# Hybrid decoder layer on one core: all projections first, then attention and output projection of the next 512 tokens emitted between the feed-forward of the current 512

## The chip, the cores and the metric

The kernel runs on one core of one Trainium2 chip. The metric is device time in microseconds (us), the median of several runs. Engines are called as the profile calls them: PE is TensorE, PEld its weight loads, DVE is VectorE, ACT is ScalarE, POOL is GpSimd, SP is SyncE, which here issues all DMAs.

## The reference

One layer over 2048 tokens of width 1024, in float32:

```python
h = rmsnorm(x, norm_mix);  proj = h @ w_in                  # 1024 x 2048
a_u, a_v, b_in, c_q, c_k, c_v, d_q, d_k, d_v = split(proj)
y_a = chunked_sgu(a_u, a_v)              # gating inside 128-token chunks
y_b = multiscale_pool(b_in)              # trailing means of 2, 4, 8, 16 tokens
y_c = sliding_window_attention(c_q, c_k, c_v)      # window 128, sinks, bias
y_d = stick_breaking_attention(d_q, d_k, d_v)      # causal, over all 2048 keys, 4 heads of 64
x = x + rmsnorm_per_mixer(concat(y_a, y_b, y_c, y_d)) @ w_out     # 1024 x 1024
h = rmsnorm(x, norm_ffn);  gate, up = split(h @ w_gate_up)         # 1024 x 5632
x = x + (silu(gate) * up) @ w_down                                 # 2816 x 1024
return rmsnorm(x, norm_final)
```

Stick-breaking weights are `sigmoid(z_ts)` times the product of `1 - sigmoid(z_tj)` over the keys between s and t: a running product along the keys, from the newest to the oldest.

## The kernel before, in words

Every product of two matrices is made of three matmuls: each operand is split into a high part and a low remainder (hi and lo), and hi*hi, hi*lo and lo*hi are summed in one PSUM bank. The split of a tile is a copy on ACT and a subtraction on POOL or DVE.

**Mixers (first 1070 us of the trace).** Three streams are written as Python generators, and `merge` (L687) emits pieces of a second stream between pieces of the first by a table of ratios (L863). The main stream is `stick` (L288): stick-breaking attention for one chunk of 512 queries and one pair of heads, eight calls. `weights` makes one block of 128 queries against 512 keys: two matmuls into a bank `z` (L300, L301), two sigmoids on ACT into `tfix` and `s` (L304, L307), a scan on DVE (L313) into `pr`, and a product `s` (L318). `turn` transposes one block of 128 keys of four such blocks (L328) into a bank `tr`, and splits it (ACT L330, DVE L331). `values` multiplies it with the values (L339, L340) into `acc`. Six `s` buffers, and two banks each for `z` and `tr`. The stream in between is `feed` (L732): projections of keys and queries of two heads, values, pooling, then the second pair of heads, spatial gating, and the third mixer's projections. Keys (`kstack`) and values (`vstack`) stay in SBUF for all 2048 tokens. After the eight calls, sliding-window attention `swa` (L419) and `out_proj` (L636) are emitted together; `out_proj` reads each 128-token tile of the mixers' results back from DRAM (`y<-yd`), norms, transposes (`ytr`) and multiplies it with the output weights, which `load_wo` (L607) splits once.

**Feed-forward (from 1070 us on).** Two blocks of 1024 tokens (L938). For each of 22 slices `f` of 128 hidden channels: `fsplit` (L904) loads and splits three weight tiles of 512 KB (`fraw`, two buffers, then `fw` in a ring of eight), 96 matmuls make gate and up (`gu`, L950), ACT and DVE form the activation (L970 to L974), and after every second slice 96 matmuls multiply with w_down (`dn`, L985) and DVE adds them to the residual `xa` (L986). `hT`, the normed tokens transposed and split, is kept for 1024 tokens.

The order on each engine is fixed when the program is built: a scheduler (`schedule_with_timeline_sim=True`) takes the emitted instructions and may take a later one first when an earlier one waits. On the chip each engine runs its list in that order.

The lines that decide where things lie:

```python
w = sb.tile([P, CH], F32, name="s", tag="dq" if spare_q else "s", bufs=4 if spare_q else 6)      # L306
ratios = (38 / 10.8, 38 / 21.6, 38 / 32.4, 52 / 43.2, 4.00, 1.20, 1.00, 1.50)                    # L863
merge(stick(c, pair, q[n]), upto(n + 2 if n < 6 else 99), ratios[n])                             # L871
ring = top.enter_context(tc.tile_pool(name="ring", bufs=8, side="left", reuse_waits="tile"))     # L874
raw = ring.tile([P, D], F32, name="fraw", tag="raw", bufs=2)                                     # L905
for blk in range(T // TB):                                                                       # L938
```

Of the kernel before, what the change touches and what calls it, by code (L numbers as in the profile page):

```python
# [15 lines left out]
P = 128  # L16
# [16 lines left out]
# column ranges of w_in  # L33
# [35 lines left out]
def _layout(inputs):  # L69
    """The arrays as the kernel reads them: slices, transposes and tiles of the inputs."""  # L70
# [33 lines left out]
TB = 1024  # L104
NT = TB // P
KS = NCH + 1
ON_G = [(7, 3)]
# [7 lines left out]
def _build(nc, tc, A, top):  # L115
    V, S, G = nc.vector, nc.scalar, nc.gpsimd
# [5 lines left out]
    dram = top.enter_context(tc.tile_pool(name="dram", bufs=1, space=bass.MemoryType.DRAM))  # L122
    yd = [dram.tile([SUB, D], F32, name=f"yd{s}") for s in range(NS)]
    vd = [dram.tile([CH, 256], F32, name=f"vd{c}") for c in range(NCH)]
    x2d = [dram.tile([CH, D], F32, name=f"x2d{c}") for c in range(NCH)]
    hn = [dram.tile([P, D], F32, name=f"hn{i}") for i in range(NT)]
    biasd = dram.tile([4, P, 384], F32, name="biasd")
    cd = [dram.tile([3, P, SUB], F32, name=f"cd{s}") for s in range(NS)]
    rbcd = [dram.tile([P, SUB], F32, name=f"rbcd{s}") for s in range(NS)]

# [5 lines left out]
    ones = const.tile([P, P], F32, name="ones")  # L136
# [8 lines left out]
    def normed(pool, x, g, out):  # L145
        """out = x * rstd(x) * g; out is scratch until then."""
        ss = pool.tile([P, 1], F32, name="fss", tag="fss", bufs=2)
        S.activation(out, x, AF.Square, accum_out=ss)
        r = pool.tile([P, 1], F32, name="fr", tag="fr", bufs=2)
        rstd(r, ss, D, pool)  # L150
        V.scalar_tensor_tensor(out, x, r, g, op0=ALU.mult, op1=ALU.mult)

    psum = top.enter_context(tc.tile_pool(name="psum", bufs=2, space=PSUM))
    rx = const.tile([P, NB], F32, name="rx")

    with ExitStack() as ph1:
        c1 = ph1.enter_context(tc.tile_pool(name="c1", bufs=1, side="left"))
        sb = ph1.enter_context(tc.tile_pool(name="sb", bufs=2, side="left"))

        stack = c1.tile([P, HD], F32, name="stack")  # L160
        tfix = [c1.tile([P, CH + 1], F32, name=f"tfix{i}") for i in range(2)]
        for t in tfix:
            G.memset(t[:, CH:CH + 1], 1.0)
        tcount = [0]
        kstack = [c1.tile([P, KS, CH], F32R, name=f"kstack{h}") for h in range(2)]
        vstack = c1.tile([P, NB, 2, P], F32R, name="vstack")

# [1 line left out]
        spare = []  # L169

        def raw_tile(shape, name):
            if spare and name == "wraw":
                tag, n = spare.pop(0)
                return sb.tile(shape, F32, name=name, tag=tag, bufs=n)
            return pp.tile(shape, F32, name=name, tag="raw", bufs=3)

        def stats(s):
            """rstd of the 256 tokens of sub-chunk s: a column of rx a block, and a row on all partitions."""
            ss = pp.tile([P, 2], F32, name="ss")
            for i in range(2):  # L180
                b = 2 * s + i
                xt = raw_tile([P, D], "xt")
                load(xt, A["x"][b * P:(b + 1) * P, :])
                S.activation(xt, xt, AF.Square, accum_out=ss[:, i:i + 1])
            r = rx[:, 2 * s:2 * s + 2]
            rstd(r, ss, D, pp)
            bc = psum.tile([P, CH], F32, name="bc", tag="ms", bufs=1)
            for i in range(2):
                dg = pp.tile([P, P], F32, name="dg", tag="k1")
                V.tensor_scalar(dg, ident, rx[:, 2 * s + i:2 * s + i + 1], None, op0=ALU.mult)  # L190
                nc.tensor.matmul(bc[:, i * P:(i + 1) * P], ones, dg, start=True, stop=True)
            rbc = pp.tile([P, SUB], F32, name="rbc", tag="rbc", bufs=2)
            S.copy(rbc, bc[:, :SUB])
            load(rbcd[s], rbc)
            return rbc

        def stored_stats(s):
            rbc = pp.tile([P, SUB], F32, name="rbc", tag="rbc", bufs=2)
            load(rbc, rbcd[s])
            return rbc  # L200

        def make_h(s, on_v=()):
            """The 256 tokens of sub-chunk s: two tiles of four channel blocks, hi and lo."""
            tok = slice(s * SUB, (s + 1) * SUB)
            out = []
            for q in range(2):
                xr = raw_tile([P, 4, SUB], "xr")
                load(xr, A["xT"][q * CH:(q + 1) * CH, tok].rearrange("(k p) t -> p k t", p=P))
                h = pp.tile([P, 4, 2, SUB], F32R, name="h", tag="h", bufs=4)
                S.copy(h[:, :, 0], xr)  # L210
                (V if q in on_v else G).tensor_tensor(h[:, :, 1], xr, h[:, :, 0].bitcast(F32), op=ALU.subtract)  # L211
                out.append(h)
            return out

# [1 line left out]
        def split_w(src, name, tag="w", bufs=4, eng=G, k0=0, step=KT):  # L216
            """src: channel blocks k0 on of [P, k, n] in DRAM; returns the hi and lo tile [P, 2, k, n]."""
            _, kt, n = src.shape
            w = (fa if tag == "wv" else pp).tile([P, 2, kt, n], F32R, name=name, tag=tag, bufs=bufs)
            per = min(kt, D // n, step)  # L220
            for k in range(0, kt, per):
                raw = raw_tile([P, per, n], "wraw")
                load(raw, src[:, k:k + per])
                g = gmix[:, k0 + k:k0 + k + per].rearrange("p (k o) -> p k o", o=1).broadcast_to([P, per, n])
                V.tensor_tensor(raw, raw, g, op=ALU.mult)
                S.copy(w[:, 0, k:k + per], raw)
                eng.tensor_tensor(w[:, 1, k:k + per], raw, w[:, 0, k:k + per].bitcast(F32), op=ALU.subtract)
            return w

        banks = ["mm", "mm", "z", "z", "tr", "tr"]  # L230

        def bank_of():
            return psum.tile([P, CH], F32, name="ps", tag=banks.pop(0) if banks else "mm")

        def proj_cm(h, w):
            ps = bank_of()
            o = ps[:, :SUB]
            for k in range(KT):
                hk = h[k // 4][:, k % 4]
                nc.tensor.matmul(o, w[:, 0, k], hk[:, 0], start=k == 0, stop=False)  # L240
                nc.tensor.matmul(o, w[:, 0, k], hk[:, 1], start=False, stop=False)  # L241
                nc.tensor.matmul(o, w[:, 1, k], hk[:, 0], start=False, stop=k == KT - 1)  # L242
            return o

        def proj_tm(h, w, n, i):
            """w(k, u): the hi (u = 0) or lo columns of channel block k."""
            ps = bank_of()
            o = ps[:, :n]
            t = slice(i * P, (i + 1) * P)
            for k in range(KT):  # L250
                hk = h[k // 4][:, k % 4, :, t]
                nc.tensor.matmul(o, hk[:, 0], w(k, 0), start=k == 0, stop=False)  # L252
                nc.tensor.matmul(o, hk[:, 0], w(k, 1), start=False, stop=False)  # L253
                nc.tensor.matmul(o, hk[:, 1], w(k, 0), start=False, stop=k == KT - 1)
            return o

# [1 line left out]
        def scaled(ps, rbc):  # L258
            t = pp.tile([P, SUB], F32, name="sc", tag="k1")
            V.tensor_tensor(t, ps, rbc, op=ALU.mult)  # L260
            return t

        def dup_q(t, outs, cols):
            """[hi; hi] and [lo; lo] of both heads in a channel-major pair."""
            for h in range(2):
                q = outs[h]
                r = slice(h * HD, h * HD + HD)
                o = slice((1 - h) * HD, (1 - h) * HD + HD)
# [19 lines left out]
        def stick(c, pair, q):  # L288
# [45 lines left out]
            def values(h, j, kb, r, wt):  # L334
# [6 lines left out]
                if j == 0 and kb == 3:  # L341
                    finish(h)
# [669 lines left out]
```

## Time and profile before

| what | value |
|---|---|
| device time, median of 3 runs | 2550.84 us (2548.78 to 2551.43) |
| profiled execution, span from first to last instruction | 2542.3 us |
| what lies around the span (median less span) | 8.5 us |
| PE busy | 2381.7 us (94%), 11836 matmuls |
| DVE, ACT, POOL busy | 1313.0 us (52%), 827.2 us (33%), 670.3 us (26%) |
| chain that ended last: PE, DVE, DMA, issue, ACT | 70%, 15%, 5%, 4%, 3% |
| mean granted TensorE clock | 0.971 |
| HBM read, written | 162.31 MB, 36.44 MB |

The profiled execution's own device time is not listed beside its span; the 8.5 us are taken from the median of the runs. A "busy" PE is one whose matmuls' modelled spans cover the time: matmuls overlap, so the distance from one start to the next says what a matmul costs, not its duration.

### The profile page before, as it was taken

To read this page: it belongs to the slowest core of one execution; us is meant where nothing else is said; L and a number is where in the kernel's file an instruction comes from. 1 tells how busy PE (TensorE), PEld (TensorE's weight loads), DVE (VectorE), ACT (ScalarE), POOL (GpSimd) and SP (SyncE) were. 2 spreads that over 40 slices of the span, in tenths; PEclk is the share of its full clock that TensorE was granted. 3 is DMA by queue.
4 is the path that set the end of the run, shared out by engine and by line. 5 is a ranking of instruction groups with operands and counts; after the bars stand their busy time and mean duration, and the time that the engine had idled before them with its cause. 6 is when DMAs were issued, how large, how long until landed. Compare 5 with 4: busy or idle time off the path is not lost.

```text
span 2542.3 us, 30367 instructions
## 1 busy us (share of the span) xinstructions
PE 2381.7 (94%) x11836; PEld 2003.2 (79%) x11836; DVE 1313.0 (52%) x2010; ACT 827.2 (33%) x1708; POOL 670.3 (26%) x504
## 2 busy tenths in 40 slices
PE   6989798887986889999999999999999999999998
PEld 6978677776865777888888888888788888888886
DVE  6788999898874554233333333333533333333335
ACT  5465566664653443222221111112411111111112
POOL 4232444553421211132222122222211222222210
PEclk9989999998996999999999999999999999999999
DMA  6241311222214333342221111111611111111101
GB/s 209 65 132 64 101 44 32 62 73 92 92 41 156 107 110 130 137 177 84 83 88 45 50 50 50 50 50 47 219 35 49 50 50 50 50 50 43 49 25 67
DMA packets 100480, 200.72 MB, mean 79 GB/s; under 512 B 8656, under 2 KB 64368, under 8 KB 100336
## 3 DMA queue, kind: packets, MB, share of 16 engines
q1 hardware_dynamic: 100336, 198.78, 23.7%
q8 instruction: 93, 1.52, 0.2%
q14 instruction: 51, 0.42, 0.1%
HBM read 162.31 MB, written 36.44 MB: 78 GB/s over the span
## 4 chain that ended last, share of the span: by engine, by line
PE 70%; DVE 15%; DMA 5%; issue 4%; ACT 3%; POOL 2%; SPq 0%; POOLq 0%; DVEq 0%; ACTq 0%
PE gu L950 38%; PE dn L985 19%; DVE pr L313 4%; DVE s L318 2%; PE ops L676 2%; PE ops L677 2%; PE ops L678 2%; DVE wt L331 1%; PE ps L240 1%; PE ytr L628 1%; PE ps L242 1%; PE ps L241 1%; PE ps L252 1%; PE ps L253 1%; ACT block L465 1%
## 5 line engine op out<-in xcount | busy, mean ns | idle before, releaser
L950 PE MATMUL gu<-hT,fw 128*128 128x512 f32 x4224 | 992.6, 390 | 0.0
L950 PEld LDWEIGHTS gu<-hT,fw 128*128 128x128 f32 x4224 | 792.5, 188 | 166.7
L909 POOL TENSOR_TENSOR fw<-fraw,fw 128x1024 fp32r<-128x1024 f32 x132 | 315.6, 2397 | 1033.0 <-ACT fw L908 1033.0
L985 PE MATMUL dn<-fw,act 128*128 128x512 f32 x2112 | 525.8, 395 | 1.4 <-DVE xa L986 0.8
L986 DVE TENSOR_TENSOR xa<-dn,xa 128x512 f32<-128x512 f32 x352 | 240.6, 689 | 551.4 <-PE dn L985 550.9
L985 PEld LDWEIGHTS dn<-fw,act 128*128 128x128 f32 x2112 | 394.8, 188 | 97.8 <-DVE xa L986 2.3
L908 ACT CAST fw<-fraw 128x1024 fp32r<-128x1024 f32 x132 | 138.6, 1053 | 562.3 <-issue 342.1
L970 ACT ACTIVATE sg<-gu 128x512 f32<-128x512 f32 x88 | 48.0, 595 | 549.4 <-PE gu L950 549.4
L972 DVE TENSOR_TENSOR sg<-gu,sg 128x512 f32<-128x512 f32 x88 | 56.7, 683 | 222.3 <-PE gu L950 222.3
L211 POOL TENSOR_TENSOR h<-xr,h 128x1024 fp32r<-128x1024 f32 x47 | 122.3, 2611 | 110.8 <-ACT h L210 108.4
L974 DVE TENSOR_TENSOR act<-sg,act 128x512 fp32r<-128x512 f32 x88 | 129.9, 1514 | 23.8 <-ACT act L973 23.6
L313 DVE TENSOR_TENSOR_SCAN pr<-tfix,cr 128x513 f32<-128x513 f32 x96 | 134.3, 1406 | 11.2 <-ACT tfix L304 11.0
L971 DVE TENSOR_TENSOR sg<-gu,sg 128x512 f32<-128x512 f32 x88 | 56.9, 686 | 121.7 <-ACT sg L970 121.6
L318 DVE TENSOR_TENSOR s<-s,pr 128x512 f32<-128x512 f32 (+3 forms) x152 | 117.1, 780 | 5.1 <-ACT s L307 1.2
L328 PE MATMUL tr<-ident,s 128*128 128x128 f32 x544 | 95.2, 279 | 12.8 <-DVE wt L331 7.1
L676 PE MATMUL ops<-wo,yT 128*128 128x512 f32 x256 | 102.1, 400 | 2.0 <-ACT yT L630 1.8
L677 PE MATMUL ops<-wo,yT 128*128 128x512 f32 x256 | 101.2, 395 | 0.0
L304 ACT ACTIVATE tfix<-z 128x512 f32<-128x512 f32 (+3 forms) x160 | 86.0, 538 | 45.0 <-PE z L301 31.9
L678 PE MATMUL ops<-wo,yT 128*128 128x512 f32 x256 | 100.4, 396 | 0.0
L330 ACT CAST wt<-tr 128x512 fp32r<-128x512 f32 (+3 forms) x160 | 81.8, 530 | 56.4 <-PE tr L328 53.2
L331 DVE TENSOR_TENSOR wt<-tr,wt 128x512 fp32r<-128x512 f32 (+3 forms) x160 | 93.3, 597 | 9.5 <-ACT wt L330 9.0
L328 PEld LDWEIGHTS tr<-ident,s 128*128 128x128 f32 x544 | 68.8, 143 | 25.5 <-issue 9.0
(194 smaller groups left out, 3523.2 us busy)
## 6 DMA issues: line engine op xcount, KB each, us to landing
fraw<-in_w_gu SPq DMA_DIRECT2D x88, 512.0 KB
xr<-in_xT SPq DMA_DIRECT2D x48, 512.0 KB
fraw<-in_w_down SPq DMA_DIRECT2D x44, 512.0 KB
xt<-in_x SPq DMA_DIRECT2D x16, 512.0 KB
xres<-in_x SPq DMA_DIRECT2D x16, 512.0 KB
y<-yd SPq DMA_DIRECT2D x16, 512.0 KB
x2d<-xres SPq DMA_DIRECT2D x16, 512.0 KB
xa<-x2d SPq DMA_DIRECT2D x16, 512.0 KB
```

The costliest lines, as they stand in the source:

```text
L313: V.tensor_tensor_scan(pr[:, c0:][:, ::-1], t[:, c0:][:, ::-1], t[:, c0:][:, ::-1], carry[h][i], op0=ALU.mult, op1=ALU.bypass)
L318: (G if (4 * pair + c, i) in ON_G else V).tensor_tensor(w[:, c0:], w[:, c0:], pr[:, c0 + 1:], op=ALU.mult)
L328: nc.tensor.transpose(tr[:, i * P:(i + 1) * P], wq[i][:, col:col + P], ident)
L676: nc.tensor.matmul(ps, yk[:, 0, :], wo[k][:, 0, cs], start=k == 0, stop=False)
L677: nc.tensor.matmul(ps, yk[:, 0, :], wo[k][:, 1, cs], start=False, stop=False)
L678: nc.tensor.matmul(ps, yk[:, 1, :], wo[k][:, 0, cs], start=False, stop=k == KT - 1)
L908: S.copy(w[:, 0], raw)
L909: G.tensor_tensor(w[:, 1], raw, w[:, 0].bitcast(F32), op=ALU.subtract)
L950: nc.tensor.matmul(pss[u][n], ws[u][:, wi, sl], hT[:, k, hi, n * CH:(n + 1) * CH], start=k == 0 and wi == 0 and hi == 0, stop=k == KT - 1 ...
L974: V.tensor_tensor(a[n][:, 1], sg, a[n][:, 0].bitcast(F32), op=ALU.subtract)
L985: nc.tensor.matmul(ps, l, r, start=j == 0, stop=j == len(m) - 1)
L986: V.tensor_tensor(xa[i][:, cs], ps, xa[i][:, cs], op=ALU.add)
```

## The change

- Keys, queries and values of all four heads of stick-breaking attention are projected in one first pass over the tokens, with pooling, and go to DRAM (`kd`, `qd`, `vv`). A second pass projects the sliding-window operands and makes spatial gating. Nothing of the attention is emitted in the first pass; attention of the first 512 tokens is merged into the second pass.
- `attention(c)` is sliding-window attention (`swa`) and both pairs of `stick` for 512 tokens; it fetches keys, queries and values from DRAM (`kst`, `dq`, `vst`, two buffers each).
- `out_proj(c)` takes 512 tokens at a time and loads and splits the output weights again for each chunk, from the feed-forward's ring.
- The feed-forward runs over four chunks of 512 tokens in place of two blocks of 1024, so its weights are loaded and split four times. Between its pieces `merge` emits `attention(c + 1)` and `out_proj(c + 1)`; what is left of these is emitted before the last `dn` group.
- PSUM banks: `mm` 3, `dn` 2, and one each of `z`, `tr` and `acc`. The ring has 7 buffers.

The core of the diff:

```diff
-TB = 1024
+BANKS = {"mm": 3, "dn": 2, "z": 1, "tr": 1, "acc": 1}
...
-    w = sb.tile([P, CH], F32, name="s", tag="dq" if spare_q else "s", bufs=4 if spare_q else 6)
+    w = sb.tile([P, CH], F32, name="s", tag="s", bufs=6)
...
+    second = second_pass(first_pass())
+    for cost in second:
+        if cost < 0:
+            break
+    first_att = attention(0, "left")
+    merge(second, first_att, 0.75)
+    for _ in first_att:
+        pass
+    ph1.close()
...
-        ring = top.enter_context(tc.tile_pool(name="ring", bufs=8, side="left", reuse_waits="tile"))
+    ring = top.enter_context(tc.tile_pool(name="ring", bufs=7, side="left", reuse_waits="tile"))
...
+    def out_proj(c, hT=None):
...
+            for half in range(2):
...
+                for kk in range(0, KT, 2):
+                    raw = ring.tile([P, 2, CH], F32, name="oraw", tag="raw", bufs=2)
+                    load(raw, A["w_out"][kk * P:(kk + 2) * P, cs].rearrange("(k p) n -> p k n", p=P))
+                    w = ring.tile([P, 2, 2, CH], F32R, name="wo", tag="w")
...
+    def feed_forward(c, hT, out):
+        xa, acts = [], []
+        for f in range(NF):
+            pss = []
+            for u in range(2):
+                w = fsplit(A["w_gu"][f, :, u].rearrange("p k m -> p (k m)"))
+                ps = bank("mm", "gu")
...
+            if f == NF - 1 and c + 1 < NCH:
+                yield -1.0
+                out.append(new_hT())
...
+    def beside(c):
+        yield from attention(c, "right")
+        yield from out_proj(c)
+
+    for c in range(NCH):
+        out = []
+        fill = beside(c + 1) if c + 1 < NCH else iter(())
+        main = feed_forward(c, hT, out)
...
+        merge(paced(), fill, (0.37, 0.44, 0.50, 0.0)[c])
```

What this does to the order, at the places of which the prediction speaks. On PE before, the feed-forward (`gu`, `dn`) follows the whole of the mixers:

```order
L678 MATMUL ops<-wo,yT 128x512
L950 MATMUL gu<-hT,fw 128x512 x192
L985 MATMUL dn<-fw,act 128x512 x6
L950 MATMUL gu<-hT,fw 128x512 x21
L985 MATMUL dn<-fw,act 128x512 x6
```

On PE with the change, in the feed-forward of the first chunk, in its fourteenth slice, where the attention of the second chunk is half done (`z`, `tr`, `acc` are stick's blocks, turns and values):

```order
L823 MATMUL gu<-hT,fw 128x512 x19
L315 MATMUL z<-kst,dq 128x512
L316 MATMUL z<-kst,dq 128x512
L823 MATMUL gu<-hT,fw 128x512 x3
L342 MATMUL tr<-ident,s 128x128
L315 MATMUL z<-kst,dq 128x512
L316 MATMUL z<-kst,dq 128x512
L353 MATMUL acc<-wt,vst 128x512
L342 MATMUL tr<-ident,s 128x128 x3
L354 MATMUL acc<-wt,vst 128x512
L315 MATMUL z<-kst,dq 128x512
L316 MATMUL z<-kst,dq 128x512
```

Up to here attention stood between runs of `gu` and `dn`; after the run of three it stands alone until the output projection.

The end of that stretch on PE, with the last turns of the attention, its `yp`, and the output projection of the same chunk (`ytr`, `ops`):

```order
L353 MATMUL acc<-wt,vst 128x512
L342 MATMUL tr<-ident,s 128x128 x4
L354 MATMUL acc<-wt,vst 128x512
L353 MATMUL acc<-wt,vst 128x512
L354 MATMUL acc<-wt,vst 128x512
L360 MATMUL yp<-stack,accs 128x64 x4
L158 MATMUL ytr<-ident,y 128x128 x8
L783 MATMUL ops<-wo,yT 128x512
L784 MATMUL ops<-wo,yT 128x512
```

The stretch has 117 matmuls from the last `gu` before it to the first `ops`. In the feed-forward of the second and third chunk the same stretch has 165 and 314. No `gu` or `dn` stands in any of them, and none between `yp` and the first `ops`.

## Rows read from the trace of the kernel before

**Rows 1.** First line of the page.

```profile
span 2542.3 us, 30367 instructions
```

**Rows 2.** Busy time by stretch: us of PE, PEld, DVE, ACT, POOL; PEclk, DMA share, GB/s.

```profile
0.00:1070.00 1070.00, 920.86 (x5436) 808.81 (x5437) 786.40 (x1305) 556.75 (x1289) 345.08 (x350) 0.93 0.29 95
1070.00:2542.30 1472.30, 1460.80 (x6401) 1194.41 (x6400) 526.60 (x705) 270.46 (x419) 325.23 (x155) 1.00 0.20 68
```

**Rows 3.** Chain of waits in order of time, feed-forward: start us, us, what.

```profile
1432.88 10.89 PE gu L950 x48
...
1498.88 10.89 PE gu L950 x48
```

**Rows 4.** Busy time by stretch, attention beside projections.

```profile
200.00:600.00 400.00, 345.71 (x1999) 298.68 (x1997) 371.02 (x590) 234.22 (x507) 172.33 (x150) 0.94 0.21 65
```

**Rows 5.** Timeline of PE: start us, us, engine, line, operation, tiles, shape, count.

```profile
18.00 0.28 PE L241 MATMUL ps<-h,w_q 128*128 128x256 f32 x1
...
19.91 0.28 PE L242 MATMUL ps<-h,w_q 128*128 128x256 f32 x1
20.04 0.34 PE L253 MATMUL ps<-w_v,h 128*128 128x384 f32 x1
...
24.82 0.34 PE L253 MATMUL ps<-w_v,h 128*128 128x384 f32 x1
...
798.06 1.04 PE L628 MATMUL ytr<-ident,y 128*128 128x128 f32 x8
...
949.80 0.39 PE L676 MATMUL ops<-wo,yT 128*128 128x512 f32 x1
...
953.67 0.39 PE L678 MATMUL ops<-wo,yT 128*128 128x512 f32 x1
```

**Rows 6.** Timeline of DVE at the end of stick, where little else runs.

```profile
737.11 0.67 DVE L318 TENSOR_TENSOR s<-s,pr 128x512 f32<-128x512 f32 x1
737.71 1.27 DVE L313 TENSOR_TENSOR_SCAN pr<-tfix,cr 128x513 f32<-128x513 f32 x1
738.91 0.65 DVE L331 TENSOR_TENSOR wt<-tr,wt 128x512 fp32r<-128x512 f32 x1
739.49 1.27 DVE L313 TENSOR_TENSOR_SCAN pr<-tfix,cr 128x513 f32<-128x513 f32 x1
...
744.34 0.69 DVE L331 TENSOR_TENSOR wt<-tr,wt 128x512 fp32r<-128x512 f32 x1 [0.45 <-ACT wt L330]
745.54 0.69 DVE L331 TENSOR_TENSOR wt<-tr,wt 128x512 fp32r<-128x512 f32 x1 [0.51 <-ACT wt L330]
```

**Rows 7.** Timeline: a mixer's result to DRAM, back, and into the output projection.

```profile
780.42 0.42 SPq L119 DMA_DIRECT2D yd<-block  x1
...
784.83 0.33 SPq L119 DMA_DIRECT2D y<-yd  x1
...
788.47 0.39 ACT L645 ACTIVATE junk<-y 128x256 f32<-128x256 f32 x1 [2.08 <-DMA y<-yd]
...
799.34 0.50 PE L676 MATMUL ops<-wo,yT 128*128 128x512 f32 x1 [0.24 <-ACT yT L630]
```

**Rows 8.** Timeline of SP: issues into one `fraw` buffer while the ring fills.

```profile
1104.40 0.33 SPq L119 DMA_DIRECT2D fraw<-in_w_gu  x1
...
1112.17 0.33 SPq L119 DMA_DIRECT2D fraw<-in_w_down  x1
```

**Rows 9.** Busy time by stretch, the start.

```profile
0.00:20.00 20.00, 9.33 (x50) 9.03 (x51) 12.12 (x17) 10.71 (x14) 7.76 (x10) 1.00 0.83 283
...
40.00:60.00 20.00, 11.41 (x62) 10.89 (x62) 15.35 (x37) 12.29 (x24) 7.59 (x8) 0.83 0.66 214
```

**Rows 10.** Busy time by stretch: the output projection beside sliding-window attention.

```profile
920.00:1000.00 80.00, 76.65 (x424) 64.23 (x425) 38.31 (x77) 34.48 (x99) 7.93 (x10) 1.00 0.36 117
```

**Rows 11.** One line's instructions: duration ns min/median/max; the activation's remainder on DVE.

```profile
L974 DVE TENSOR_TENSOR act<-sg,act x88: 677/688/2489, 1093.2 to 2510.6; 128x512 fp32r<-128x512 f32 x88
```

**Rows 12.** Busy time by stretch: the tail of stick, PE thinly used.

```profile
750.00:760.00 10.00, 5.93 (x19) 4.47 (x19) 3.70 (x7) 5.34 (x17) 2.20 (x4) 0.56 0.08 26
```

More of the change, by code (lines that the diff above doesn't have):

```diff
@@ L135, in _build, with bank @@
     ident = const.tile([P, P], F32, name="ident")
-    ones = const.tile([P, P], F32, name="ones")
+    stack = const.tile([P, HD], F32, name="stack")
+    gout = const.tile([P, KT], F32, name="gout")
+    def bank(tag, name):
+        return psum.tile([P, CH], F32, name=name, tag=tag, bufs=BANKS[tag])
     def rstd(out, ss, n, pool):
@@ new lines, in raw_tile, with stats @@
+    def raw_tile(shape, name):
+        return pp.tile(shape, F32, name=name, tag="raw", bufs=5)
+    def stats(s):
+        ss = pp.tile([P, 2], F32, name="ss")
+        for i in range(2):
+            b = 2 * s + i
+            xt = raw_tile([P, D], "xt")
+            load(xt, A["x"][b * P:(b + 1) * P, :])
+            S.activation(xt, xt, AF.Square, accum_out=ss[:, i:i + 1])
+        r = rx[:, 2 * s:2 * s + 2]
+        rstd(r, ss, D, pp)
+        bc = bank("dn", "bc")
+        for i in range(2):
+            dg = pp.tile([P, P], F32, name="dg", tag="k1")
+            V.tensor_scalar(dg, ident, rx[:, 2 * s + i:2 * s + i + 1], None, op0=ALU.mult)
+            M.matmul(bc[:, i * P:(i + 1) * P], ones, dg, start=True, stop=True)
+        rbc = pp.tile([P, SUB], F32, name="rbc", tag="rbc", bufs=2)
+        S.copy(rbc, bc[:, :SUB])
+        load(rbcd[s], rbc)
+        return rbc
@@ new lines, in make_bias @@
+    def make_bias():
+        work = raw_tile([P, D], "bwork")
+        oh, rb, lh, om = work[:32, :384], work[:32, 896:900], work[:32, 768:896], work[:, 384:768]
+        load(rb, A["rel_bias"])
+        load(oh, A["c_onehot"])
+        load(om, A["c_outside"].broadcast_to([P, 384]))
+        for h in range(4):
+            V.tensor_copy(lh, rb[:, h:h + 1].broadcast_to([32, P]))
+            bp = bank("dn", "bp")
+            M.matmul(bp[:, :384], lh, oh, start=True, stop=True)
+            bs = raw_tile([P, 384], "bs")
+            V.tensor_tensor(bs, bp[:, :384], om, op=ALU.add)
+            load(biasd[h], bs)
@@ new lines, in out_proj, with fsplit @@
+            for i in range(4):
+                b = 4 * c + i
+                load(x2d[b], xr[i])
+                r = row_rstd(op, xr[i])
+                n = op.tile([P, D], F32, name="xn", tag="y")
+                V.scalar_tensor_tensor(n, xr[i], r, gffn, op0=ALU.mult, op1=ALU.mult)
+                if hT is None:
+                    load(hn[b], n)
+                else:
+                    split_T(n, halves(hT, i), ("acc", "dn"))
+                yield 0.1
+    def fsplit(src):
+        raw = ring.tile([P, D], F32, name="fraw", tag="raw", bufs=2)
+        load(raw, src)
+        w = ring.tile([P, 2, D], F32R, name="fw", tag="w")
+        S.copy(w[:, 0], raw)
+        G.tensor_tensor(w[:, 1], raw, w[:, 0].bitcast(F32), op=ALU.subtract)
+        return w
```

1214 lines of the change are left out of this document (521 added, 693 removed).

## The prediction

> **What bounds the kernel now.** I read the stretches first. The trace falls into two parts [rows 2]: 1070 us of mixers in which PE is busy 86% of the time at a granted clock of 0.93, and 1472 us of feed-forward in which it is busy 99% at 1.00. Then I asked what the feed-forward costs if nothing holds it. In the chain of waits the same run of 48 `gu` comes again after 1498.88 - 1432.88 = 66.0 us [rows 3]; two slices lie between, 192 `gu` and 96 `dn`, so a matmul of 512 columns starts every 66.0 / 288 = 0.229 us. The 6336 of them make 1452 us, and 1472 were taken. The feed-forward is PE-bound with 20 us left over for its ends. The mixers are not: from 200 to 600 us DVE is busy 93% (371 of 400) and PE 86% [rows 4].
>
> So I priced all of PE's work by the distance between starts, not by busy time. A projection of 256 columns starts every (19.91 - 18.00) / 16 = 0.119 us, one of 384 every (24.82 - 20.04) / 27 = 0.177 us, one of 512 every (953.67 - 949.80) / 17 = 0.228 us, and eight transposes take 1.04 us, of which the last ends 0.27 after its start, so 0.11 us each [rows 5]. With the counts of the order: 6336 x 0.229 = 1452; 1152 of 512 (768 `ops`, 384 gating) 262; 1728 of 256 206; 384 of 384 68; stick's 448 wide `z` and `acc` 102 and 192 narrower ones 26; some 1470 transposes and matmuls of 64 or 128 columns at 0.11, 161; 120 of the sliding window 14. The sum is **2290 us**. The span is 2542.3 [rows 1], so 252 us of it are PE idle or slow, nearly all in the mixers. The change leaves the matmuls what they are: the order has the same PE instructions by kind and number. It can only gain from these 252 us, and it is faster if what it leaves uncovered is less than 252 us.
>
> **The change, part by part, by what it leaves uncovered.**
>
> Start. In the first 20 us PE has 9.3 busy, from 40 to 60 11.4 [rows 9], together 19 idle. The first pass waits for the same loads and splits: **20**.
>
> The two passes, 214 and 163 us of PE. Without stick, DVE has about 18 us of work for a sub-chunk of 256 tokens, PE 27, so DVE no longer bounds. Nothing lost is the lower bound, the 13.6% idle of [rows 4] (51 us) the upper. I take 5%, nearer to the lower, since DVE was what filled those rows: **19**.
>
> Attention of the first chunk is merged into the second pass, but the order has its last ten turns behind all projections; about 21 us for 9 of PE: **13** (5 to 20).
>
> First output projection, which nothing accompanies. A result goes to DRAM at 780.42, is read back from 784.83, is there at 788.47, and the first product starts at 799.34 [rows 7]: 19 us in which PE has a few transposes. Behind the last product its four tiles are added, squared, normed, transposed and split before the first `gu`, as ACT takes 1.6 us a tile for the squares and 1.2 for the copies: 15. Together **34**.
>
> The stretches in which attention stands alone. Here the order speaks: the feed-forward's weights and the output weights share a ring of seven, the output weights are emitted before attention is through, and the feed-forward stops two slices later. From there to `yp` lie 14, 20 and 38 turns, 72 of stick's 160, with 60 blocks, and 93 us of PE. DVE's steps are 0.60 us from a product to the scan, 1.20 for the scan, 0.58 for the remainder [rows 6]. So DVE's floor is 48 wide blocks at 1.8, 12 narrow ones at about 1.2 and 72 remainders at 0.6: 143 us, 50 of them without PE. A turn that runs alone took 1.20 us [rows 6] with two `tr` banks; with one, transposes, copy and remainder follow each other, 0.55 + 0.6 + 0.6 and the signals between, 1.9. And a turn needs all four blocks of its group, while six `s` buffers let only two of the next be made ahead. So a group of four turns takes some 10.5 us rather than DVE's 9.6, and 18 groups 190: **97** uncovered. The upper end is 235, with PE at half clock, 142 uncovered.
>
> The step from attention to `ops`, three more times, with no feed-forward in between in the order. The same 19 us [rows 7]: **57** (36 if only the two transfers and the first norm count).
>
> Ends of the feed-forward. Before, one change of block and one tail made 20 us. Now there are three changes and a shorter tail: **24**.
>
> Attention between the feed-forward's matmuls elsewhere. The nearest stretch is the output projection beside the sliding window, 4.2% idle [rows 10]; of some 800 us this would be 34. The feed-forward's runs are longer, so 25; none is the lower bound, and 13.6% [rows 4], 109, the upper: **25**.
>
> What is hidden: 132 more weight tiles are loaded, copied on ACT and subtracted on POOL. While the ring filled, one `fraw` buffer took 1112.17 - 1104.40 = 7.8 us from issue to issue [rows 8]; two buffers give a tile every 3.9 us, and PE uses one in 24 x 0.229 = 5.5. If that cover failed, the whole feed-forward would run at the feed's pace. The 24 more tiles of output weights of 512 KB come through the same buffers. The trip of keys, queries and values through DRAM adds 96 fetches, which the order has a group ahead; SP's list grows from 509 to 818 issues at about 0.33 us [rows 8], 270 us of 2590. In each step to `ops` SP waits at the write of `yd` with `y`, `xres` and the next weights queued behind; their users wait for `ops` anyway. ACT loads its tables 18 times rather than 6, on an engine busy a third of the time. Sixteen fewer input tiles are split, also beside PE.
>
> The sum: 2290 + 20 + 19 + 13 + 34 + 97 + 57 + 24 + 25 = 2579 us of span. The median of the runs lies 8.5 above the profiled span before, so **2588 us**, 1.5% slower. The uncovered 289 stand against 252 before: the mixers' idle time is spent less, but the feed-forward, which lost nothing, now loses some 200.
>
> **The rivals.**
>
> Faster. The stretches go at DVE's floor: 143 in place of 190 (47 less), the steps to `ops` take 12 in place of 19 (28 less for four), the passes lose nothing (19 less). Then 2588 - 94 = 2494. For it: at the end of stick DVE ran block after block without idle time [rows 6]. Against it: `z` and `tr` have one bank now and had two. It decides on the group of four turns: with the rest as summed, it must fall from 10.5 to about 8.5 us before the total meets 2551, which is under the floor of a full group, so the steps or the passes must give too.
>
> Half clock. Where stick tailed off and PE had 19 matmuls in 10 us, the granted clock was 0.56 [rows 12]; alone, stick gives PE about 30 in 10 us. At 1.2 GHz the stretches take 235 (45 more), and each of four steps is followed by some 5 us at that clock (20 more): 2653.
>
> POOL against DVE. The activation's remainder takes 0.68 us, but up to 2.49 [rows 11], which is 1.8 longer, and a weight's subtraction on POOL takes 2.4. With twice as many of these, DVE's operations beside the feed-forward end later, and PE, whose order is fixed, waits for them. If 44 of 88 remainders and 40 of the 84 products of stick made there wait 1 us each in PE's path, the time is 2588 + 84 = 2672. The Trainium skill, SBUF — State Buffer, section "Who interferes with whom", says that a DVE instruction with two SBUF inputs and a POOL instruction that reads SBUF exclude each other for the whole instruction. By that rule the delay is the rest of a POOL subtraction, as the 2.49 shows it; by a rule that shared bandwidth evenly, no remainder would take 0.68 and another 2.49.
>
> That the change does not do what it says is in the forecast already: 72 of 160 turns do not run beside the feed-forward.
>
> **How the numbers follow.** A measurement of this kernel can tell about 0.2%, 5 us, from no change. Forecast, 2546 to 2630 around 2588: 0.35. Faster rival: 0.35, since each of its three parts is a sum of steps that may overlap more than I let them. Half clock: 0.18. POOL: 0.12. Of the forecast and the faster rival 0.03 each lie within 0.2% of 2551. So faster 0.32, same 0.06, slower 0.62. The range reaches down to 2500, which leaves out the lower third of the faster rival (0.12), and up to 2680, which leaves out the upper half of the POOL case and a bad half clock (0.08). The forecast's own range is 2546 to 2630.
>
> **What would show it.** In the profile after: a first part of some 480 us with PE busy 90% or more and DVE below 70%; then feed-forward with three stretches of about 36, 53 and 100 us without `gu`, in which DVE is busy over 80%; behind each, about 19 us in which PE does almost nothing but transposes, up to a `y` load; a last 370 us at 0.229 us a matmul. I am wrong if the feed-forward of the first three chunks takes under 490 us on the mean, if `fw` waits for `fraw` while PE waits for `fw`, if the passes take over 430 us, or if PE's idle time beside the feed-forward is put down to single remainders or products of DVE.

## The result, and the profile after

The changed kernel took **2735.2 us** (median of 4 runs, 2733.41 to 2737.01) against 2550.68 us before: a ratio of 1.0724 (95% interval 1.0708 to 1.0739), 7.2% slower. The forecast was 2588 with a range of 2500 to 2680. The sign was right; the size was not, and none of the rivals gave this time.

The page's first line and the busy time by stretch show where it went (columns: us, busy time of PE, PEld, DVE, ACT, POOL, then PEclk, DMA share, GB/s). They answer to [rows 1, 2].

```profile
span 2731.7 us, 31511 instructions
```

```profile
0.00:515.00 515.00, 446.11 (x2909) 414.43 (x2910) 309.99 (x598) 199.99 (x371) 184.85 (x155) 0.94 0.43 138
515.00:602.60 87.60, 62.33 (x265) 48.86 (x265) 40.44 (x60) 39.54 (x88) 24.20 (x15) 0.79 0.62 214
602.60:640.00 37.40, 24.34 (x89) 18.85 (x90) 7.28 (x9) 5.16 (x7) 8.74 (x9) 0.77 0.25 76
640.00:861.80 221.80, 221.29 (x1074) 183.94 (x1073) 126.61 (x161) 95.53 (x180) 88.75 (x66) 1.00 0.34 111
...
1078.00:1129.00 51.00, 30.98 (x122) 24.75 (x121) 10.81 (x15) 8.96 (x12) 16.00 (x10) 0.83 0.30 93
...
1658.00:1705.00 47.00, 25.13 (x86) 19.68 (x85) 9.80 (x12) 7.38 (x9) 10.57 (x9) 0.71 0.25 79
1705.00:2031.20 326.20, 325.19 (x1556) 268.51 (x1554) 201.35 (x247) 141.56 (x265) 130.86 (x81) 1.00 0.37 121
2031.20:2165.00 133.80, 90.70 (x326) 56.05 (x325) 91.74 (x117) 68.33 (x159) 11.76 (x19) 0.78 0.20 66
...
2370.00:2731.70 361.70, 352.63 (x1553) 290.78 (x1551) 145.15 (x167) 91.14 (x119) 145.82 (x64) 0.99 0.30 97
```

The reader is to see three things. Feed-forward with attention between its matmuls (640 to 862, 1705 to 2031) keeps PE over 99% busy, so the weave itself works. The last chunk, feed-forward alone in 512 tokens, takes 362 us for 1553 matmuls, 0.233 each, where the feed-forward before took 1472 for 6401, 0.230 each; four loads of the weights cost next to nothing. In the feed-forward, time is lost in short pieces between: where the sliding-window attention of the next 512 tokens begins (602 to 640, 1078 to 1129, 1658 to 1705; called heads from here on), and in the stretches before each output projection (one of them 2031 to 2165), in which no engine is busy throughout. The second and third head do not stand at the start of a chunk of the feed-forward but near its end: 919 of its 1056 `gu` have started there, and the scheduler has taken the next attention's first steps ahead.

Measured as the prediction did, a stretch loses its time less the matmuls started in it at the prediction's prices. On that scale PE's 11836 matmuls, the same in both kernels, make 2292 us; 440 us are lost after and 250 before.

| what is lost by PE, us | predicted | measured |
|---|---|---|
| the two passes, first attention and its tail (to 515) | 52 | 105 |
| first output projection, with the step to it | 34 | 36 |
| the three heads | in the 25 below | 69 |
| stretches in which attention stands alone | 97 | 138 |
| step to `ops`, and `ops` itself, three times | 57 | 68 |
| attention between the matmuls elsewhere, and the ends of three chunks | 25, and 24 with the end below | 17 |
| last chunk and its end (from 2370) | | 6 |

**The heads**, which the prediction did not have. Timelines of PE, ACT and DVE at the second of them (start us, us, what; in brackets idle time before and its releaser):

```profile
1087.94 4.59 PE L852 MATMUL dn<-fw,act 128*128 128x512 f32 x12 [4.33 <-DVE xa L853]
1092.37 4.47 PE L823 MATMUL gu<-hT,fw 128*128 128x512 f32 x19
1112.53 4.42 PE L852 MATMUL dn<-fw,act 128*128 128x512 f32 x12 [15.69 <-DVE xa L853]
```

```profile
1084.75 0.83 ACT L202 CAST ck<-kr 128x768 fp32r<-128x768 f32 x1 [6.61 <-DMA kr<-cd]
...
1109.34 0.83 ACT L202 CAST ck<-kr 128x768 fp32r<-128x768 f32 x1 [23.24 <-DMA kr<-cd]
1110.07 0.59 ACT L834 ACTIVATE sg<-gu 128x512 f32<-128x512 f32 x1
```

```profile
1110.20 0.95 DVE L203 TENSOR_TENSOR ck<-kr,ck 64x768 fp32r<-64x768 f32 x1 [21.71 <-ACT ck L202]
...
1111.79 1.28 DVE L853 TENSOR_TENSOR xa<-dn,xa 128x512 f32<-128x512 f32 x2
```

PE waits 15.69 us for `xa`, the residual's addition, which frees a `dn` bank. `xa` itself waits for nothing: it stands on DVE behind the split `ck` of the next attention's sliding-window keys, which waits for ACT, which waits 23.24 us for a DMA (`kr<-cd`). ACT's sigmoid (`sg`) and, through ACT's copies, POOL's weight splits stand behind the same transfer. The transfer is what is slow. DMA view of 1083 to 1097 us, 40 slices (busy tenths, then GB/s):

```profile
DMA  1111115899731111111111111115366111111111
GB/s 47 44 44 47 41 47 105 287 386 369 298 105 47 41 47 47 41 47 44 44 61 47 47 47 47 50 47 159 98 205 203 45 44 47 41 47 47 41 47 44
```

Weights come at 287 to 386 GB/s; the keys and queries of the sliding window come at 41 to 50, with a tenth of the 16 DMA engines busy. The kernel before has the same rate around 800 us, and I had not looked at this view there:

```profile
DMA  7999997999953111011111111131289997311111
GB/s 280 348 389 352 321 280 280 321 319 333 352 201 113 55 55 55 41 55 55 43 41 50 48 48 48 48 102 48 75 266 393 362 375 266 116 65 48 48 48 48
```

**The stretches.** Who made PE's transposes wait, over the whole run (the page's view of line L342, the `tr` of attention's turns):

```profile
  DVE wt L345: 74.7, 103
...
  DVE s L332: 16.7, 22
```

In 103 places the next turn's transposes wait until DVE has read the one `tr` bank (`wt`), often behind a scan (1.46 us on the mean). **The step to `ops`**, answering to [rows 7], at the last stretch (timelines of PE, SP, ACT):

```profile
2152.19 1.10 PE L360 MATMUL yp<-stack,accs 128*128 128x64 f32 x8 [0.68 <-ACT accs L357]
2164.04 1.94 PE L158 MATMUL ytr<-ident,y 128*128 128x128 f32 x8 [10.74 <-DVE y L761]
```

```profile
2153.73 0.89 SPq L117 DMA_DIRECT2D yd<-ysb  x2
2155.67 0.33 SPq L117 DMA_DIRECT2D y<-yd  x1
```

```profile
2159.25 0.42 ACT L756 ACTIVATE junk<-y 128x256 f32<-128x256 f32 x1 [5.54 <-DMA y<-yd]
```

From the last `yp` to the first `ytr` PE stands still for 11 us, three times; from the write of `yd` to the first `ops` it is 12 us here, where the forecast had 19, and some 10 more are lost in `ops` itself, which it did not have. **The activation's remainder**, answering to [rows 11], is now slow in most of its 88 executions: the median rose from 688 to 2366 ns.

```profile
L838 DVE TENSOR_TENSOR act<-sg,act x88: 678/2366/2526, 635.9 to 2712.4; 128x512 fp32r<-128x512 f32 x88
...
  PEld dn L852: 2.7, 4
  PE dn L852: 0.9, 2
```

The last two lines say who waited for it directly (us, times): PE for under 4 us in all.

### The profile page after: what moved, and what is told of

Read it like the earlier page. It is cut to its first block, busy times and chain, and to the rows that moved or that the text cites. A ratio compares the mean times of both kernels' runs of the same rounds, so it can differ in the third digit from the quotient of the medians.

```text
span 2731.7 us, 31511 instructions
## 1 busy us (share of the span) xinstructions
PE 2452.4 (90%) x11836; PEld 2023.0 (74%) x11836; DVE 1425.5 (52%) x2012; ACT 1011.8 (37%) x1892; POOL 927.4 (34%) x617
## 4 chain that ended last, share of the span: by engine, by line
PE 66%; DVE 12%; DMA 8%; issue 5%; ACT 3%; POOL 3%; SPq 3%; DVEq 0%; POOLq 0%; ACTq 0%
PE gu L823 30%; PE dn L852 16%; SPq L117 3%; PE tr L342 2%; DVE pr L327 2%; PE ops L783 2%; DMA kr<-cd 2%; PE ops L785 2%; PE ops L784 2%; DMA fraw<-in_w_gu 1%; POOL fw L806 1%; DVE s L332 1%; PE ps L475 1%; PE ps L476 1%; PE ps L477 1%
## 5 line engine op out<-in xcount | busy, mean ns | idle before, releaser
L823 PE MATMUL gu<-hT,fw 128*128 128x512 f32 x4224 | 1035.7, 392 | 1.4 <-ACT hT L160 0.7
L806 POOL TENSOR_TENSOR fw<-fraw,fw 128x1024 fp32r<-128x1024 f32 x264 | 641.4, 2435 | 960.5 <-ACT fw L805 919.4
L852 PE MATMUL dn<-fw,act 128*128 128x512 f32 x2112 | 551.4, 399 | 44.5 <-DVE xa L853 43.5
L805 ACT CAST fw<-fraw 128x1024 fp32r<-128x1024 f32 x264 | 275.9, 1049 | 458.5 <-DMA fraw<-in_w_gu 162.1
L838 DVE TENSOR_TENSOR act<-sg,act 128x512 fp32r<-128x512 f32 x88 | 170.3, 1935 | 71.4 <-ACT act L837 71.3
L327 DVE TENSOR_TENSOR_SCAN pr<-tfix,cr 128x513 f32<-128x513 f32 x96 | 139.9, 1458 | 28.1 <-ACT tfix L319 27.3
L342 PE MATMUL tr<-ident,s 128*128 128x128 f32 x544 | 112.9, 319 | 41.0 <-DVE wt L345 32.7
L342 PEld LDWEIGHTS tr<-ident,s 128*128 128x128 f32 x544 | 74.3, 160 | 81.0 <-DVE wt L345 42.1
L836 DVE TENSOR_TENSOR sg<-gu,sg 128x512 f32<-128x512 f32 x88 | 60.6, 689 | 137.3 <-PE gu L823 136.9
L437 POOL TENSOR_TENSOR h<-xr,h 128x1024 fp32r<-128x1024 f32 x31 | 76.3, 2473 | 128.7 <-ACT h L436 128.1
L835 DVE TENSOR_TENSOR sg<-gu,sg 128x512 f32<-128x512 f32 x88 | 60.7, 690 | 106.7 <-ACT sg L834 106.5
L783 PE MATMUL ops<-wo,yT 128*128 128x512 f32 x256 | 105.4, 415 | 0.6 <-ACT wo L775 0.3
L784 PE MATMUL ops<-wo,yT 128*128 128x512 f32 x256 | 103.9, 407 | 0.0
L785 PE MATMUL ops<-wo,yT 128*128 128x512 f32 x256 | 103.0, 406 | 0.0
```

The source lines that it names most:

```text
L327: V.tensor_tensor_scan(pr[:, c0:][:, ::-1], t[:, c0:][:, ::-1], t[:, c0:][:, ::-1], carry[h][i], op0=ALU.mult, op1=ALU.bypass)
L342: M.transpose(tr[:, i * P:(i + 1) * P], wq[i][:, col:col + P], ident)
L783: M.matmul(pss[i], yk[:, 0, t], w[:, k, 0], start=first, stop=False)
L784: M.matmul(pss[i], yk[:, 0, t], w[:, k, 1], start=False, stop=False)
L785: M.matmul(pss[i], yk[:, 1, t], w[:, k, 0], start=False, stop=last)
L805: S.copy(w[:, 0], raw)
```

## The experiments

Eleven kernels ran. The first eight begin from the changed kernel or build on each other.

**E1, a second buffer for the raw keys.**

```diff
-                kr = fa.tile([P, 2, P + SUB], F32, name="kr", tag="kr", bufs=1)
+                kr = fa.tile([P, 2, P + SUB], F32, name="kr", tag="kr", bufs=2)
```

> One edit: two buffers in place of one for the sliding window's raw keys (kr). In the changed kernel (2735.2 us) each of the three chunk heads has DVE and ACT wait for kr before the split ck (PE loses 11, 16 and 14 us at the second split of each pair). Theory 'one buffer': the second load starts only when the first split is done; with two buffers the second wait goes at each head, 30 to 40 us: 2695 to 2705. Rival 'slow transfers': the loads of 1 KB rows themselves move at some 45 GB/s one behind the other, so the second lands little earlier: 2720 to 2732. If neither, and the head is a matter of weights: 2735.

Measured: 2738.2 us, no change. PE still waits 14.3 us at the second split of the second head. The buffer is not the cause. The number lies nearest the last guess, a matter of weights; E5 decides against that. SP's issues go at the pace of the transfers: four of them, two of 128 KB and two of 64, hold it for 11.03 us, in which the queue, several transfers in flight, moves 45 GB/s (timeline of SP; DMA view of 1096.3 to 1107.3, whose last number is the share of the 16 DMA engines):

```profile
1096.29 11.03 SPq L117 DMA_DIRECT2D kr<-cd  x4
...
DMA packets 504, 0.49 MB, mean 45 GB/s; under 512 B 10, under 2 KB 488, under 8 KB 504
...
q1 hardware_dynamic: 504, 0.49, 13.5%
```

**E2, a second `tr` bank, and E3, a bank of its own for the output projection.** Each takes one of the three `mm` banks; passes use it under its new name.

```diff
-BANKS = {"mm": 3, "dn": 2, "z": 1, "tr": 1, "acc": 1}
+BANKS = {"mm": 2, "dn": 2, "z": 1, "tr": 2, "acc": 1}              # E2
+BANKS = {"mm": 2, "dn": 2, "z": 1, "tr": 1, "acc": 1, "op": 1}     # E3
...
-                tags = ("acc", "tr", "z", "dn") if c or half else ("mm", "mm", "mm", "dn")
+                tags = ("acc", "tr", "z", "dn") if c or half else ("mm", "mm", "tr", "dn")   # E2
+                tags = ("acc", "tr", "z", "op")                                             # E3
```

> One PSUM bank moves from the feed-forward's gate and up (mm 3 to 2) to attention's turns (tr 1 to 2); first-pass projections use the same three banks under two names. Theory 'one tr bank sets the pace': a turn in the stretches in which attention stands alone falls from 3.26 us (234.6 us for 72 turns) to 2.4 to 2.6, the order's stretches shrink to some 47 turns, 115 us in place of 235, of which PE work is 60: 2640 to 2680. Rival 'DVE's work and the fixed order set the pace': 3.0 us or more a turn, and only the fewer turns count: 2690 to 2710. Rival 'two mm banks are too few': gate and up wait for the activation in every slice, the last chunk takes over 375 us (362 now): over 2735.

Measured: 2674.5 us, 61 less. PE's sums lie in banks of PSUM, and here a bank is taken again once ACT and DVE have read it. The three stretches of the changed kernel and of E2 by stretch (columns as above), each from the last `gu` or `dn` to the last `yp`:

```profile
861.80:906.50 44.70, 32.43 (x113) 20.00 (x111) 28.72 (x41) 21.73 (x48) 3.64 (x8) 0.77 0.09 30
1451.70:1515.90 64.20, 45.15 (x160) 27.18 (x158) 43.06 (x58) 31.40 (x67) 3.73 (x8) 0.78 0.10 33
2031.20:2152.20 121.00, 88.65 (x314) 54.10 (x312) 90.18 (x114) 63.88 (x142) 9.93 (x17) 0.80 0.14 45
```

```profile
881.70:903.60 21.90, 17.35 (x60) 12.25 (x59) 14.08 (x21) 9.34 (x19) 0.00 (x0) 0.69 0.12 39
1466.30:1490.30 24.00, 16.80 (x65) 10.54 (x63) 17.18 (x24) 12.18 (x24) 0.00 (x0) 0.79 0.11 33
2020.10:2096.30 76.20, 59.21 (x231) 40.73 (x228) 64.11 (x81) 44.20 (x99) 5.64 (x9) 0.82 0.16 45
```

By the `acc` products in them these are 78 turns in 229.9 us, 2.95 a turn, and 46 in 122.1, 2.65 a turn (by the order's own counts, 72 and 47, they are 3.19 and 2.60); DVE's share rose from 70% to 78%. The wait of the transposes for `wt` is gone:

```profile
  DVE s L332: 32.7, 36
...
  DVE wt L345: 0.2, 1
```

So the bank count sets part of the pace and, through the order, most of the number of turns that stand alone. The granted clock in the stretches is no higher (0.69 to 0.82 against 0.77 to 0.80), so the gain is not one of clock. Two `mm` banks are enough for the feed-forward: the last chunk, from its first `gu`, takes 370 us in both. What PE loses in the stretches fell by 75 us; before the first `gu` it lost some 10 more.

> One PSUM bank moves from the feed-forward's gate and up (mm 3 to 2) to the output projection, which so holds none of the feed-forward's two dn banks; all else as in the changed kernel. Theory 'the bank stops the feed-forward': the order has 48 turns in the stretches in place of 72, so 24 turns at 3.26 us less the PE work of 1.3 go: 45 to 55 us, 2680 to 2690, the pace of a turn staying at 3.2. Rival 'the shared weight ring stops it' (what the prediction held): no change of the stretches, 2725 to 2740.

Measured: 2698.6 us, 37 less, and less than the 45 to 55 expected. The order has 48 turns alone where it had 72, and the stretches last 138 us; they lose some 80 us where they lost 138, but PE's loss from the first `gu` on falls by 32 only (299 to 267), so the rest came back as waits elsewhere. The prediction had the ring of weights as what stops the feed-forward. The output projection's fourth product does so too: it holds one of two `dn` banks that the feed-forward takes in turn. E6 below tells the two apart.

**E4, cost between attention and the output projection** (30 us in the merge's reckoning).

```diff
         yield from attention(c, "right")
+        for _ in range((0, 60, 60, 60)[c]):
+            yield 0.5
         yield from out_proj(c)
```

> A cost of 30 us is put between attention's last piece and the output projection's first in the merge, so that some 60 to 80 us more of feed-forward are emitted between the two. The order then has 2, 16 and 32 turns alone in place of 14, 20 and 38. Theory 'attention alone is what costs': 22 turns fewer at 2 us each uncovered, 44 us: 2685 to 2700. Rival 'attention lags the merge in any case, the lag only moves': under 15 us, 2720 to 2740.

Measured: 2736.6 us, no change, and a miss of the first theory. The stretches did lose less, some 90 us in place of 138, but as much came back elsewhere: from the first `gu` on PE loses 299 us in both. Some 15 of it stand at the ends of two chunks, where the transposes of the next chunk's normed tokens now wait, as the output projection comes later.

**E5, the same bytes by transfers with 64 rows as their outer dimension.** Edited likewise for the other `kr` and the `qr` loads:

```diff
-                    load(kr[:, g, P:], both_halves(cd[s][0, g * HD:(g + 1) * HD, :]))
+                    for u in range(2):
+                        load(kr[u * HD:(u + 1) * HD, g, P:], cd[s][0, g * HD:(g + 1) * HD, :])
```

> One edit to the changed kernel (2735.2 us): the sliding window's keys and queries (kr, qr), which one transfer fetches for both halves of the partitions (an outer dimension of 2), are fetched by two transfers of 64 rows each. In the trace these transfers run at some 44 GB/s with a tenth of the 16 DMA engines busy, and each of the three chunk heads loses about 20 us of PE behind them. Theory 'the outer dimension of 2 keeps a transfer on two DMA engines': the rate rises several times, the splits come in time, and 50 to 60 us go at the heads and up to 10 in the second pass: 2670 to 2690. Rival 'rows of 1 KB are slow in any form': 44 GB/s as before and two times the issues, 2735 to 2750.

Measured: 2652.5 us, **83 less**, more than I had put on it. The DMA view of the same place (1047 to 1062 us there), and the first two heads by stretch:

```profile
DMA  8999897959767644109789866600093999785363
GB/s 339 339 396 328 298 341 210 206 198 328 319 247 236 219 145 122 45 0 197 208 339 404 328 200 205 191 27 0 0 153 66 360 371 385 251 262 156 101 134 87
```

```profile
591.70:640.00 48.30, 48.29 (x213) 40.07 (x214) 21.41 (x23) 12.50 (x15) 22.29 (x18) 0.97 0.37 110
1030.00:1100.00 70.00, 70.00 (x311) 57.94 (x310) 30.44 (x38) 21.06 (x26) 35.72 (x20) 1.00 0.51 163
```

PE is busy throughout at the heads now, and the stretches are as they were. The view, weights included, has 219 GB/s on the mean where that of the changed kernel has 90. The transfers were slow through their form, not through rows of 1 KB, and not through too few in flight, as E1's queue shows. The Trainium skill, DMA: Bandwidth & Descriptors, section "Rules for kernel authors", says so: a leading broadcast dimension of c copies confines a transfer to c engines at most. The trace agrees with c = 2: two of 16 engines are 12.5%, and E1's 11 us, nearly all such transfers, show 13.5%.

**E6, both causes at once**, and the output projection's fourth product in a `tr` bank, so that it holds no `dn` bank.

```diff
+                tags = ("acc", "tr", "z", "tr") if c or half else ("mm", "mm", "tr", "dn")
```

> Three edits together: the 64-row transfers, a second tr bank out of mm, and the output projection's fourth product in that tr bank in place of one of the feed-forward's two dn banks. The order has 1 and 8 turns alone (second and third stretch) and none in the first, where the changed kernel has 14, 20 and 38. Theory 'what the bank count and the transfers cost is the whole difference to before': 138 us lost in stretches fall to 20, 60 lost at heads to 10, steps and passes stay: 2735 - 118 - 50 = 2567, 2550 to 2590. Rival 'attention between the matmuls then waits there' (PE's idle time moves from the stretches to single waits beside the feed-forward): 2600 to 2640.

Measured: 2555.9 us, ratio to before 1.0025 (1.0015 to 1.0036). The 179 us that went are close to the sum of three edits measured alone (83 + 61 + 37 = 181); that E2 and E3 add up, though both take turns out of the same stretches and E3 has another bank, is not explained. The ring still has seven buffers, yet 9 turns stand alone where 72 did: the banks stopped the feed-forward, and not the ring. From the first `gu` on, PE now loses 133 us in place of 299:

```profile
0.00:597.60 597.60, 509.16 (x3172) 464.26 (x3172) 348.47 (x657) 236.77 (x457) 209.32 (x170) 0.93 0.46 150
597.60:2560.40 1962.80, 1873.54 (x8664) 1534.87 (x8664) 1098.26 (x1355) 764.39 (x1434) 722.98 (x447) 0.98 0.36 117
```

**E7, the activation's remainder on POOL**, on top of E6.

```diff
-            V.tensor_tensor(a[:, 1], sg, a[:, 0].bitcast(F32), op=ALU.subtract)
+            G.tensor_tensor(a[:, 1], sg, a[:, 0].bitcast(F32), op=ALU.subtract)
```

> As the run with the three edits, and the activation's remainder (1.94 us mean on DVE, 0.69 at least) goes to POOL. Theory 'POOL and DVE in each other's way': DVE is freed of 170 us of work in all and of the waits behind it, the attention beside the feed-forward follows closer: 20 to 40 us less than the run with the three edits. Rival 'PE's order decides, DVE has room': within 8 us of it. Against both: the remainder comes later on POOL, behind a weight's 2.4 us subtraction, and dn waits for it: slower by 10 or more.

Measured: 2539.3 us, 17 less than E6, just short of what was expected. On POOL the remainder takes 1.30 us in nearly every execution:

```profile
L843 POOL TENSOR_TENSOR act<-sg,act x88: 1270/1295/2267, 611.0 to 2515.0; 128x512 fp32r<-128x512 f32 x88
```

**E8, the cost of E4 on top of E6** (25, 25 and 20 us).

> As the run with the three edits, and 25, 25 and 20 us of cost between attention and output projection in the merge. Theory 'the step from attention to the output projection (12 us idle, three times) is covered when feed-forward stands between': 20 to 35 us less than the run with the three edits. Rival, as the gap alone did in the changed kernel: the output projection moves to the end of its chunk, where the next chunk's normed tokens are late, and it gives back what it gained: within 8 us.

Measured: 2518.6 us, 37 less than E6, where a like edit gave nothing in the changed kernel. With the banks free, feed-forward does stand between attention and the output projection, and of the three steps of 11 us one is left, in the third chunk:

```profile
2032.65 1.94 PE L158 MATMUL ytr<-ident,y 128*128 128x128 f32 x8 [10.68 <-DVE y L766]
```

**E9, the kernel before with the edit of E5.**

> The kernel before with the one edit of the 64-row transfers. There the sliding window's fetches run at the same 44 to 50 GB/s in the trace, around 800 us, beside the output projection. Theory 'the slow transfers were hidden in the kernel before and are not in the changed one': within 5 us of 2550, 2545 to 2555. Rival 'they cost the kernel before as well' (its mixers lose 63 us of PE from 760 to 1070): 2500 to 2535.

Measured: 2510.5 us against 2548.4 in the same series, ratio 0.9854 (0.9840 to 0.9868): **the kernel before loses 38 us to the same transfers.** Its output projection beside the sliding window shortens by all of it. The kernel before, then E9, from 760 us to their first `gu`:

```profile
760.00:1070.00 310.00, 268.59 (x1416) 228.04 (x1417) 139.65 (x271) 121.97 (x345) 47.67 (x69) 0.91 0.36 120
```

```profile
760.00:1032.00 272.00, 257.35 (x1399) 219.05 (x1400) 141.40 (x268) 120.03 (x338) 47.59 (x66) 0.96 0.40 132
```

I had expected them to be hidden there; they were not.

**E10 and E11, towards the best version.** E10 is E6 with both E7 and E8; E11 changes three numbers of E10:

```diff
-        for _ in range((0, 50, 50, 40)[c]):
+        for _ in range((0, 50, 50, 60)[c]):
...
-    merge(second, first_att, 0.75)
+    merge(second, first_att, 1.1)
...
-        merge(paced(), fill, (0.37, 0.44, 0.50, 0.0)[c])
+        merge(paced(), fill, (0.37, 0.44, 0.56, 0.0)[c])
```

> The three edits (64-row transfers, second tr bank, dn banks left to the feed-forward) with both the cost put before the output projection and the activation's remainder on POOL. If the two gains (37 and 17 us, each measured on top of the three edits) are of different waits, they add up: 2500 to 2505. If both only take attention's lag away: 2512 to 2518, as the cost alone.

Measured: 2502.0 us, ratio 0.9816 (0.9802 to 0.9829): the gains add up. It is faster than the kernel before by 1.8%, but than E9, the kernel before with its transfers alone mended, by 0.3% only.

> As the run before it, with a faster merge in the third chunk (0.56 for 0.50, with 30 us of cost in place of 20, so that feed-forward stands between attention and the last output projection) and the first attention merged into the second pass at 1.1 in place of 0.75. If the last uncovered step (17 us of PE idle around 2020 us) and the tail of the passes (480 to 520 us, 23 us lost) are what is left: 10 to 25 us less than the run before it, 2480 to 2495. If attention's lag grows with its faster emission: within 5 us of it.

Measured: 2506.3 us, 4 more than E10. The three numbers gave nothing. That attention emitted faster lags more, as its second line had it, would fit; it is not shown.

## Why the prediction was wrong

**The bound and PE's work: right.** The matmuls are the same in kind and number, the last chunk goes at nearly the same price a matmul (0.233 us against 0.230), and the four loads of the weights are hidden, as the last chunk shows. The sum's last term, 8.5 us around the span, measured 1.7 (2733.41 less 2731.7).

**"The nearest stretch is the output projection beside the sliding window, 4.2% idle [rows 10]": the step that failed.** From it I took 25 us for all attention between the feed-forward's matmuls. That stretch, 920 to 1000, begins after the last of the sliding window's fetches in the kernel before, so it shows attention without them (views of `kr` and `qr` before; duration of an issue in ns, first and last start in us):

```profile
L119 SPq DMA_DIRECT2D kr<-cd x16: 484/978/3305, 580.1 to 886.0; - x16
L119 SPq DMA_DIRECT2D qr<-cd x32: 484/507/3605, 596.1 to 910.3; - x32
```

Nor are they under what is hidden: the 96 fetches that the prediction counts there, at 0.33 us an issue, are stick's (40 `kst`, 40 `vst`, 16 `dq`). The sliding window's keys and queries come in a form that runs at some 44 GB/s, and their splits stand on ACT, DVE and POOL ahead of the feed-forward's own operations. What I priced at 25 measured 86: 69 at the heads and 17 elsewhere. That is inside the 109 that I gave as the upper end, but for a cause that I did not have. E5 took 83 us off the time; between the two profiled executions PE's loss fell by 65 from the first `gu` on and by 11 before it. The rate was to be read in the DMA view of the kernel before, which loses 58 us from 760 to 920 and, with E9's edit, 24: part of the 252 us that I took as given.

**The stretches: the mechanism right, the size off.** "18 groups 190: 97 uncovered" measured 230 and 138. I had one `tr` bank at 1.9 us a turn that runs alone, but gave the group 10.5 us; with transposes waiting behind scans it took 230 / 18 = 12.8. With a second bank (E2) it is 4 x 2.60 = 10.4, so this is the bank. That the ring of weights stops the feed-forward was wrong: the banks did (E3, E6). The steps, 57, came out at 68, but made otherwise: 12 us each where I had 19, and 10 more in each `ops`.

**The passes: 52 predicted, 105 measured, above even the upper end of 91.** With them at 515 us, the sign "if the passes take over 430 us" came true. "I take 5%, nearer to the lower, since DVE was what filled those rows." The bound itself was too low: it took PE's idle share in [rows 4], 13.6%, but by the prediction's own prices those 400 us lose 90, 22.5%, as their matmuls also ran slower, at a granted clock of 0.94. So here: PE is idle for 69 of the 515 us, and the other 36 are matmuls that took longer than priced, again at 0.94. The idle time is mostly short waits in many places; thirteen of over 1 us make 44. The longest is for `dg`, whose tokens (`xt`) SP fetched only after the stores of `biasd`, at 130.27. This was read from the trace and not tried; some 11 us of it may be slow transfers (E5), and for the rest the cause stays open. The timelines of PE and SP there:

```profile
139.69 1.22 PE L417 MATMUL bc<-dg,ones 128*128 128x128 f32 x4 [10.55 <-DVE dg L416]
```

```profile
122.70 5.70 SPq L117 DMA_DIRECT2D biasd<-bs  x3
...
130.27 0.92 SPq L117 DMA_DIRECT2D xt<-in_x  x2
```

**The rivals.** POOL against DVE is real, as the remainder's 2366 ns show, and worth 17 us on top of E6 (E7; not tried on the changed kernel itself), not 84: PE waits for the remainder directly for under 4 us. Half clock alone would have given 2653. Its 235 us for the stretches were nearly met, by 230, but not for its reason: their granted clock was 0.77 to 0.80, and E2 shortened them at no better clock. The faster rival's DVE floor was not met by any run in the stretches: DVE reached 78% in E2.

**What the change is worth.** With the transfers alone mended, the changed order takes 2652 us (E5) and the order before 2510 (E9). With all its mends the changed order is 0.3% under that (E10); whether the remainder on POOL, one of them, would help the order before as well was not tried. By the scale above E10 loses 208 us, 133 of them before its first `gu`; E9 loses 198 before its first `gu` and 15 behind it. So what interleaving takes from the mixers' idle time stays in the passes, the first output projection and what is left of the steps.

## What to carry to other kernels

When work is moved beside a PE-bound stretch, look at each operand fetch it brings with it: its rate in the DMA view, and what stands behind its first user on every in-order engine; a slow load stops ACT, DVE, POOL and PE in turn. A transfer with a broadcast of two as its outer dimension is better written as two transfers: here that was worth 83 us in one order and 38 in the other. Count what each side of an interleave holds of the other's banks before counting cycles: one bank given to the transposes was worth 61 us here, one given to the output projection 37.

## What the runs showed of the hardware that I had not expected

Transfers of 64 and 128 KB in two broadcast halves ran at 41 to 50 GB/s with a tenth of the DMA engines busy, and held SP behind them, up to 3.8 us for an issue where others take 0.33; with each as two transfers of 64 rows the same place, weights included, moved 219 GB/s on the mean in place of 90. The activation's remainder on DVE took 2.37 us in the median beside twice as many POOL subtractions (0.68 at least), and 1.30 on POOL itself.
